# The first MLP product of a hybrid attention block in seven half-size products, with weight sums made by adding DMAs and an order planned inside the kernel

## The chip, the core and the metric

The kernel runs on one core of a Trainium2 chip. The metric is the device time of one launch in microseconds (us). The program is compared with itself before the change. The engines have short names throughout: PE is TensorE (its weight loads are listed apart as PEld), DVE is VectorE, ACT is ScalarE, POOL is GpSimd, and SP is SyncE, which issues most of the transfers.

## The reference

One layer works on 512 tokens of 1024 features, all in float32. The part that the change touches is the last line but one.

```python
def reference(x, positions, g_mix, w_in, ..., g_mlp, w_ff1, w_ff2, g_final):
    h = x
    n = rmsnorm(h, g_mix)
    proj = n @ w_in                     # 512 x 1024 times 1024 x D_IN
    y_gla = gla_branch(...)             # gated linear attention, both directions
    y_mla = mla_branch(...)             # attention over low-rank keys and values, 8 heads
    merged = sigmoid(z_ma) * y_gla + sigmoid(z_mb) * y_mla
    h = h + merged @ w_out              # 1024 x 1024
    m = rmsnorm(h, g_mlp)
    h = h + square(relu(m @ w_ff1)) @ w_ff2   # 1024 x 4096, 4096 x 1024
    return rmsnorm(h, g_final)
```

## The kernel before

Every float32 operand of a product is split into two parts that TensorE takes in one pass each: a high part, which ACT makes by a copy into the type fp32r, and a low part, the rest, which DVE makes by a subtraction (`split`, lines 92 to 94). One product of such pairs is three matmuls, high by high, high by low and low by high (`mm3`, lines 87 to 90):

```python
nc.tensor.matmul(acc, lh, rh, ...)   # L88
nc.tensor.matmul(acc, lh, rl, ...)   # L89
nc.tensor.matmul(acc, ll, rh, ...)   # L90
```

The kernel goes through four stages: the input projections, the two attention branches, the output projection `w_out`, and the MLP. The MLP is the last 315 us. Its input, `m` transposed, lies in eight tiles `mT`, one for each 128 features, each with high and low part for all 512 tokens. The hidden layer has 4096 features, which are 32 tiles of 128. They are worked in four groups (`qd`) of eight tiles.

**First product.** `hidden` (L1480) makes one tile: its weights (1024 x 128, 512 KB) are loaded by SP in pieces of 512 bytes into one of three staging tiles, split into one of four pairs of weight tiles, and multiplied with `mT` in 8 x 3 = 24 matmuls of 128 features by 512 tokens; ACT takes the sum out of PSUM with Relu (L1493). `pair_units` (L1496) takes two such tiles, a pair, squares them on ACT and sorts them by token halves into `px` (tokens 0 to 255) and `qx` (256 to 511) (L1502, L1503).

**Second product.** The square of the hidden layer times `w_ff2` is already made by a scheme of seven products for eight: tokens are halved, the two hidden tiles of a pair are the halves along the summed dimension, and the output columns are halved. Per pair, `left_sums` (L928) makes four sums of the quarter blocks on DVE (L933 to L936), and `split_first`, `split_sum`, `split_corner` split them and the quarter blocks into high and low parts (`ga`; `ghb`, `glb`; `ghc`, `glc`; `gd`). The weight side has four blocks B11, B12, B21, B22 of each group, loaded by `load_w2` on SP; `add_w2` (L986, L988) makes their sums on DVE in place, 32 instructions of 128 x 1024 in the whole MLP, and `prep` (L1448) says which sum is made before which product. Each of the seven block products of a group is 2 row blocks x 4 pairs x 3 = 24 matmuls of 512 columns, in the order `ORDER = (1, 5, 6, 3, 7, 4, 2)`. `add_rows` (L1425, L1427) adds a finished sum from PSUM to the output rows `h` on DVE. In the last group `last_rows` (L1549) works the last products row block by row block, so that the final norm (square on ACT, power -0.5 on POOL, scale, store) of some rows lies under the products of others; the last block is done in two column halves.

**Order.** Most instructions are put in order by the tile scheduler of the language. Where it matters the kernel fixes the order by hand: `traced()` marks a place, `in_program_order` (L110) ties every later instruction of the named engines to the one written ahead of it, and `goes_behind` (L125) moves a marked stretch behind another. Up to the first two hidden tiles (made early, `early[0]` and `early[1]`, while the output projection ends) PE, ACT and DVE go in written order. From line 1686 on, which is the loop over the four groups, the order is the scheduler's, but for the last group's tail.

**Memory.** Tiles come from rings with a fixed number of buffers: `u2` (128 x 512, 29 buffers), `u4` (128 x 2 x 512, 26), weight tiles `wh`, `wl` (4 each), staging `wf` (3). An earlier place in the program has the scans of the linear attention's gates with tiles `rr` (L458, two buffers of their own, L462 the scan).

POOL has little to do in the MLP. In the `w_out` stage it already issues ten transfers that add what they read to what lies in the tile (L984), for the sums of that product's weights.

Of the kernel before, what the change touches and what calls it, by code (L numbers as in the profile page):

```python
# [56 lines left out]
def tile_block(ctx: ExitStack, tc: tile.TileContext, t, out: bass.AP):  # L57
# [128 lines left out]

    class Flipped:
        def __init__(self, gains, name):
            self.gains, self.name = gains, name
            self.out = [u4(f"{name}T{k}") for k in range(KD)]  # L190
            self.banks = {}
# [11 lines left out]
        def evacuate(self, half, ks=range(KD)):  # L203
            tok = slice(half * 256, half * 256 + 256)
            for k in ks:
                hl = self.out[k]
                src = self.banks[half][k % 4][:, (k // 4) * 256 : (k // 4) * 256 + 256]
                split_scaled(hl[:, 0, tok], hl[:, 1, tok], src, self.gains[:, k : k + 1])
# [50 lines left out]
    R = one([P, S], F32, "R")  # L259
# [108 lines left out]

    def gated(acc, name):
# [3 lines left out]
        th = u2(f"t{name}")  # L373
        nc.scalar.activation(th, z, AF.Tanh, scale=0.5)  # L374
        return z, th
# [11 lines left out]
    g2 = [gated(f_accs[2 + x], f"b{x}")[1] for x in range(2)]  # L387
# [47 lines left out]
    class Gates:  # L435
# [492 lines left out]
    def left_sums(px, qx, name, eng):  # L928

        a11, a12, a21, a22 = px[:, 0:HT], px[:, HT:S], qx[:, 0:HT], qx[:, HT:S]  # L930
        y, z = u2(f"y{name}"), u2(f"z{name}")
        s1, s2, s3, s4 = y[:, 0:HT], y[:, HT:S], z[:, 0:HT], z[:, HT:S]
        eng.tensor_tensor(s1, a21, a22, op=ALU.add)  # L933
        eng.tensor_tensor(s2, s1, a11, op=ALU.subtract)  # L934
        eng.tensor_tensor(s3, a11, a21, op=ALU.subtract)
        eng.tensor_tensor(s4, a12, s2, op=ALU.subtract)  # L936
        return y, z

# [47 lines left out]
    def add_w2(dst, x, y, op):  # L986
        for g in range(NP // 2):
            nc.vector.tensor_tensor(wq[dst][g], wq[x][g], wq[y][g], op=op)  # L988

# [18 lines left out]
    def split_w2(x, name):  # L1008
        return [split_part(x, g, name) for g in range(NP // 2)]

    def merged_sums(p, eng):
        px, qx = merged[p]
        a11, a12, a21, a22 = px[:, 0:HT], px[:, HT:S], qx[:, 0:HT], qx[:, HT:S]
        y, z = u2(f"yo{p}"), u2(f"zo{p}")
# [154 lines left out]
    def finish_zb(f, begun):  # L1171
        g2.append(gated(proj_run(begun, xT), f"b{f}")[1])
# [147 lines left out]
    g2.append(gated(zb, "b6")[1])  # L1320
# [18 lines left out]
    g2.append(gated(proj_run(zb, xT, None, range(3, KD)), "b7")[1])  # L1339
# [108 lines left out]
    def prep(m, qd):  # L1448

        more = qd + 1 < NQ  # L1450
        name = f"b{m}_{qd}"
        if m == 1:
            return split_w2(B11, name)
        if m == 2:
            res = split_w2(B21, name)
            if more:
                load_w2(qd + 1, B21)
            return res
        if m == 3:
            return split_w2(B22, name)  # L1460
        if m == 5:
            add_w2(B11, B12, B11, ALU.subtract)
            return split_w2(B11, name)
        if m == 6:
            add_w2(B11, B22, B11, ALU.subtract)
            return split_w2(B11, name)
        if m == 7:
            add_w2(B12, B22, B12, ALU.subtract)
            res = split_w2(B12, name)
            if more:  # L1470
                load_w2(qd + 1, B12)
                load_w2(qd + 1, B22)
            return res
        add_w2(B11, B21, B11, ALU.subtract)
        res = split_w2(B11, name)
        if more:
            load_w2(qd + 1, B11)
        return res

    def hidden(qd, j):  # L1480

        if qd == 0 and j < 2:
            acc = early[j][2]
        elif qd == 0 and j in (2, 3):
            at = traced()
            begun = proj_begin(w1, j * P, f"f{qd}{j}")
            goes_behind((at, traced()), span["norm", NT - 1] if j == 2 else span["evacuate", 1], SPLITTERS)
            goes_behind((at, traced()), span["sums"], SP_ONLY)
            acc = proj_run(begun, mT)
        else:  # L1490
            acc = proj_run(proj_begin(w1, (qd * FQ + j) * P, f"f{qd}{j}"), mT)
        a = u2(f"fa{qd}{j}")
        nc.scalar.activation(a, acc, AF.Relu)  # L1493
        return a

    def pair_units(qd, p, a22):  # L1496

        px, qx = u2(f"px{qd}{p}"), u2(f"qx{qd}{p}")
        for x in range(2):
            a = hidden(qd, 2 * p + x)  # L1500
            c = slice(x * HT, (x + 1) * HT)
            nc.scalar.activation(px[:, c], a[:, 0:HT], AF.Square)  # L1502
            nc.scalar.activation(qx[:, c], a[:, HT:S], AF.Square)  # L1503
        left = {}
        split_first(left, px, f"{qd}{p}")
        y, z = left_sums(px, qx, f"{qd}{p}", nc.vector)
        split_sum(left, y, 5, 6, f"b{qd}{p}")
        split_sum(left, z, 7, 3, f"c{qd}{p}")
# [252 lines left out]
```

## Time and profile before

| | |
|---|---|
| median of three runs | 759.44 us (758.06 to 759.54) |
| the profiled execution | 758.17 us |
| its span, first to last instruction | 756.5 us |
| mean granted TensorE clock | 0.997 |
| busy in the span | PE 745.2, DVE 592.5, ACT 468.1, POOL 128.1 us |

The page of the profile has the engines' busy times, the span cut into 40 slices, the DMA queues (q1 the one with SP's plain transfers, q0 the software queue that POOL issues), the chain of work that ended last, and groups of instructions. A row of a group gives line, engine, operation, names of output and inputs, shapes and count, then the busy time and the mean duration of one in ns, then how long the engine stood idle just before these instructions and what ended that. A row of the timeline gives the start, the duration and the instruction, and in brackets the idle time before it. The shown durations of one engine can overlap: the start of the next instruction tells more of the rate than the duration does.

### The profile page before, as it was taken

How to read it: one execution, taken by the hardware profiler on the slowest of the kernel's cores; microseconds unless marked ns; L12 is line 12 of the kernel's file. 1: busy time of each engine (PE TensorE's matmuls, PEld its weight loads, DVE VectorE, ACT ScalarE, POOL GpSimd, SP SyncE). 2: the span in 40 equal slices, each digit the busy share in tenths (PEclk: the TensorE clock that was granted, in tenths of full speed). 3: DMA queues.
4: the chain of work that ended last, by engine and by line, in shares of the span. 5: the costliest groups of instructions: out<-in, count | busy, mean ns of one | idle time of the engine just before them, and what ended most of it. 6: DMA issues, size and time to landing. Idle time of an engine off the chain costs nothing.

```text
span 756.5 us, 10217 instructions
## 1 busy us (share of the span) xinstructions
PE 745.2 (99%) x3704; PEld 629.7 (83%) x3704; DVE 592.5 (78%) x887; ACT 468.1 (62%) x812; POOL 128.1 (17%) x186
## 2 busy tenths in 40 slices
PE   8999999999999999999999999999999999999996
PEld 7888788888888888899988988888888888888885
DVE  7779899687787787998897787856696578748795
ACT  7556658478767576988866766345544555345644
POOL 1620002031321115036850100000000000000014
PEclk9999999999999999999999999999999999999998
DMA  9832311312234324237998411461126410650003
GB/s 316 255 95 91 128 29 28 84 49 62 59 84 112 60 50 112 73 89 184 273 203 221 133 57 55 139 193 58 56 61 203 127 56 3 206 154 0 29 0 112
DMA packets 97075, 81.30 MB, mean 107 GB/s; under 512 B 15376, under 2 KB 74784, under 8 KB 97024
## 3 DMA queue, kind: packets, MB, share of 16 engines
q1 hardware_dynamic: 93760, 74.07, 33.1%
q0 software_dynamic: 2976, 6.05, 4.3%
q8 instruction: 29, 0.48, 0.3%
q10 hardware_dynamic: 288, 0.52, 0.2%
q14 instruction: 22, 0.18, 0.1%
HBM read 76.96 MB, written 2.10 MB: 105 GB/s over the span
## 4 chain that ended last, share of the span: by engine, by line
PE 93%; ACT 2%; DVE 2%; issue 1%; DMA 1%; POOL 0%; POOLq 0%; ACTq 0%; DVEq 0%
PE f L89 8%; PE f L88 8%; PE f L90 8%; PE gx L88 4%; PE gx L89 4%; PE gx L90 4%; PE first L329 3%; PE tp L1116 2%; PE gz L89 2%; PE gz L88 2%; PE gz L90 2%; PE zb L88 1%; PE za L88 1%; PE zb L90 1%; PE za L90 1%; PE za L89 1%
## 5 line engine op out<-in xcount | busy, mean ns | idle before, releaser
L1700 POOL DMA_DIRECT2D gfin<-in_g_final x1 | 0.6, 623 | 284.1 <-PE f L90 284.1
L988 DVE TENSOR_TENSOR w<-w,w 128x1024 f32<-128x1024 f32 x32 | 38.7, 1219 | 0.3
L1101 ACT ACTIVATE e<-s,top 128x512 f32<-128x512 f32 x32 | 21.9, 685 | 4.4 <-DVE top L1096 3.5
L94 DVE TENSOR_TENSOR pT<-tp,pT 128x512 fp32r<-128x512 f32 x32 | 21.6, 681 | 2.9 <-ACT pT L93 2.9
L1096 DVE TENSOR_REDUCE top<-s 128x1 f32<-128x512 f32 x32 | 21.6, 680 | 2.0 <-PE s L90 1.7
L1427 DVE TENSOR_TENSOR h<-h,gx 128x512 f32<-128x512 f32 x32 | 21.4, 680 | 1.9 <-PE gx L90 1.8
L93 ACT ACTIVATE pT<-tp 128x512 fp32r<-128x512 f32 x32 | 18.8, 592 | 4.3 <-PE tp L1116 4.0
L479 POOL COPY v3f<-rrf 128x4 f32<-128x4 f32 x4 | 2.8, 705 | 109.3 <-DVE rrf L462 109.3
L1116 PE MATMUL tp<-ident,e 128*128 128x128 f32 x128 | 19.3, 274 | 0.3 <-ACT e L1107 0.2
L88 PE MATMUL av<-pT,v 128*128 128x256 f32 x64 | 19.0, 298 | 0.0
L93 ACT ACTIVATE ghb<-y 128x512 fp32r<-128x512 f32 x16 | 10.1, 632 | 14.0 <-DVE y L934 14.0
L1493 ACT ACTIVATE fa<-f 128x512 f32<-128x512 f32 x32 | 18.4, 576 | 0.0
L89 PE MATMUL av<-pT,v 128*128 128x256 f32 x64 | 18.2, 285 | 0.0
L90 PE MATMUL av<-pT,v 128*128 128x256 f32 x64 | 18.2, 284 | 0.0
L1116 PEld LDWEIGHTS tp<-ident,e 128*128 128x128 f32 x128 | 15.1, 140 | 3.7 <-ACT e L1107 1.0
L93 ACT ACTIVATE b_00h<-w 128x1024 fp32r<-128x1024 f32 x7 | 7.4, 1060 | 12.6 <-PE gz L90 6.0
L93 ACT ACTIVATE b_10h<-w 128x1024 fp32r<-128x1024 f32 x7 | 7.4, 1060 | 12.1 <-PE gz L90 6.0
L93 ACT ACTIVATE b_20h<-w 128x1024 fp32r<-128x1024 f32 x7 | 7.4, 1060 | 12.1 <-PE gz L90 6.0
L88 PE MATMUL s<-kbuf,q 96*128 96x512 f32 x32 | 14.1, 441 | 0.0
L374 ACT ACTIVATE tb<-zb 128x512 f32<-128x512 f32 x8 | 5.0, 632 | 14.7 <-DVE zb L372 14.7
L1502 ACT ACTIVATE px<-fa 128x256 f32<-128x256 f32 x32 | 13.4, 418 | 1.0
L984 POOL DMA_DIRECT2D w<-in_w_out x10 | 12.2, 1397 | 6.5 <-DVE bo60l L94 5.3
(1743 smaller groups left out, 2919.1 us busy)
## 6 DMA issues: line engine op xcount, KB each, us to landing
w<-in_w_ff SPq DMA_DIRECT2D x64, 256.0 KB, 3.4
w<-in_w_out POOLq DMA_DIRECT2D x10, 512.0 KB, 8.8
grw<-in_w_in SPq DMA_DIRECT2D x8, 512.0 KB, 9.1
gvw<-in_w_in SPq DMA_DIRECT2D x8, 512.0 KB, 4.5
w<-in_w_out SPq DMA_DIRECT2D x16, 256.0 KB, 5.9
x<-in_xt SPq DMA_DIRECT2D x8, 256.0 KB, 5.3
h<-in_x SPq DMA_DIRECT2D x4, 512.0 KB, 5.1
vw<-in_w_first SPq DMA_DIRECT2D x7, 256.0 KB, 5.4
```

The source lines that it names most:

```text
L88: nc.tensor.matmul(acc, lh, rh, start=start, stop=False, skip_group_check=onto)
L89: nc.tensor.matmul(acc, lh, rl, start=False, stop=False, skip_group_check=onto)
L90: nc.tensor.matmul(acc, ll, rh, start=False, stop=stop, skip_group_check=onto)
L93: nc.scalar.activation(hi, src, AF.Copy)
L94: rest.tensor_tensor(lo, src, raw(hi), op=ALU.subtract)
L329: nc.tensor.matmul(f_accs[i], a[:, i * P : (i + 1) * P], b, start=k == 0 and x == 0, stop=k == KD - 1 and x == 2)
L988: nc.vector.tensor_tensor(wq[dst][g], wq[x][g], wq[y][g], op=op)
L1096: nc.vector.tensor_reduce(top, acc, axis=AX.X, op=ALU.max, negate=True)
L1101: nc.scalar.activation(e, acc, AF.Exp, bias=top, accum_out=tot[:, qt % 2 : qt % 2 + 1])
L1116: nc.tensor.transpose(tp[:, k * P : (k + 1) * P], e[:, k * P : (k + 1) * P], ident)
L1427: nc.vector.tensor_tensor(hc, hc, acc, op=op)
L1493: nc.scalar.activation(a, acc, AF.Relu)
```

## The change

**The first product.** Tiles 0 to 3 stay as they are, but are worked in token halves (`hidden_run`), since `m` transposed now lies in eight tiles by feature half, token half, high and low (`fm.out[j, c]`). The other 28 tiles become seven quads of four tiles. A quad (512 hidden features) uses seven products for eight: the summed dimension (1024) is halved, the tokens are halved, and the four tiles are two pairs of 256 features. One of its products is 2 feature tiles x 4 pieces of 128 x 3 = 24 matmuls of 256 columns. The sums on the token side are made once, by DVE, behind the norm (`summing`: four sums of high and low part, four combinations; `split_m` splits those four). The sums on the weight side are made once per quad: three by transfers that add (`load_add`, issued by POOL) to a loaded block, one more by a DVE addition. PSUM is emptied after every product: m1, m5 and m6 by an ACT copy, m2, m3 and m7 by a DVE addition followed by Relu and Square on ACT, m4 by Relu and Square alone.

**The second product.** Its scheme stays with other signs. The weight sums (`add_w2`, 32 DVE additions) go away; B11 and its follow-ups are made in the tile, by a chain of adding transfers, each issued once the split of the former content has read it. There are 57 adding transfers in the MLP now (two of them ahead of the plan, `w1_sums`), and 59 plain ones in the plan.

**The order.** The loop over the groups is replaced by a list of tasks. PE's order is written out: the first product of a group in pieces between the last products of the odd quad, then group products and products of the next even quad in turn, then the next odd quad. For the other engines, `Plan` makes a list schedule while the kernel is built: each task has a cost (`COST`, and figures for the landing of transfers), a latest start from PE's order, and the tasks that it must follow; at each step the earliest task that can start is taken, the more urgent one first. The instructions are then emitted in that order and tied in it for PE, ACT, DVE and POOL.

**The rest.** The split of tile 3 (with that of tile 2) stands ahead of the second evacuation of `m`. `u2` goes from 29 to 24 buffers, `u4` from 26 to 30; `R` and `rr` move into these rings, and the gates' tanh tiles share one `u4` tile by twos. In the last group the products go 1, 5, 3, 6, 2 (row block 0), 7, 2 (row block 1), 4 (row block 0), 4 (row block 1, in two column halves).

```diff
     def u2(name, dt=F32, shape=(P, S)):
-        return tl(list(shape), dt, "u2", 29, name)
+        return tl(list(shape), dt, "u2", 24, name)
 
     def u4(name, dt=F32R, shape=(P, 2, S)):
-        return tl(list(shape), dt, "u4", 26, name)
+        return tl(list(shape), dt, "u4", 30, name)
...
-    def add_w2(dst, x, y, op):
-        for g in range(NP // 2):
-            nc.vector.tensor_tensor(wq[dst][g], wq[x][g], wq[y][g], op=op)
...
-            rr = tl([P, NT, P + 1], F32, "rr", 2, f"rr{d}")
+            rr = u4(f"rr{d}", F32, (P, NT, P + 1))
...
+    def hidden_run(begun, half, ks=range(KD)):
+        wh, wl, acc = begun
+        c = slice(half * HT, (half + 1) * HT)
+        for k in ks:
+            hi, lo = fm.out[k // 4, half]
+            mm3(acc[:, c], wh[:, k, :], wl[:, k, :], hi[:, k % 4, :], lo[:, k % 4, :], k == 0, k == KD - 1)
+        return acc
...
+    for j in (2, 3):
+        begin_hidden(j)
     at = traced()
     fm.evacuate(1)
...
+        def order(self, head):
...
+                for e in free:
+                    for i in open_[e]:
+                        if e == "PE" and i != pe[0]:
+                            continue
+                        t = max(free[e], ready[i])
+                        rank = (t, late[i], i)
+                        if best is None or rank < best[0]:
+                            best = rank, e, i
...
+                if e in ("SP", "POOL") and lands:
+                    bus = max(bus, end) + 2.6
+                    end = max(bus + 2.0, end + lands)
...
+    COST = {"ACT": {FULL: 0.97, HALFT: 0.52, QUART: 0.32}, "DVE": {FULL: 1.16, HALFT: 0.62, QUART: 0.34}}
...
+    def load(dst, src, key):
+        plan.add("SP", 0.1, lambda: nc.sync.dma_start(dst, src), (), (key,), 4.5)
+
+    def load_add(dst, src, key):
+        plan.add("POOL", 1.27, lambda: nc.gpsimd.dma_start(dst, src, accum_op=ALU.add), (key,), (key,), 9.4)
...
+    wfs = Ring("wf", [stage(KD, P, f"wf{n}") for n in range(3)])
+    hls = Ring("hl", [halves(KD, P, f"hl{n}") for n in range(4)])
...
+        act(FULL, lambda: nc.scalar.activation(wh, src, AF.Copy), (key,), (hkey + (0,),))
+        dve(FULL, lambda: nc.vector.tensor_tensor(wl, src, raw(wh), op=ALU.subtract), (key, hkey + (0,)), (hkey + (1,),))
...
+                dve(FULL, (lambda x=x, hi=hi, lo=lo: nc.vector.tensor_tensor(x, raw(hi), raw(lo), op=ALU.add)),
+                    m_key_of(j, c), (key,))
...
+        combine(A, A, C, ALU.subtract)
+        combine(C, B, C, ALU.subtract)
+        combine(B, B, A, ALU.add)
+        combine(Dd, B, Dd, ALU.subtract)
...
+        def fetch(self):
...
+            load(self.a, self.rows(1, 0), ka)
+            load_add(self.a, self.rows(1, 1), ka)
+
+        def weights(self, m):
...
+            if m == 5:
+                load_add(a, self.rows(0, 0), self.ka)
+                if self.q > 1:
+                    load(self.e, self.rows(1, 0), self.ke)
+                    load_add(self.e, self.rows(0, 0), self.ke)
+            elif m == 6:
+                item, c, key = self.c
+                dve(FULL, lambda: nc.vector.tensor_tensor(a, a, c, op=ALU.add), (self.ka, key), (self.ka,))
...
+        def multiply(self, m):
...
+                for x in range(2):
+                    c = slice(x * HT, (x + 1) * HT)
+                    f = slice(x * P, (x + 1) * P)
+                    for k in range(KD // 2):
+                        mm3(acc[:, c], wh[:, k, f], wl[:, k, f], hi[:, k, :], lo[:, k, :],
+                            begin and x == 0 and k == 0, k == KD // 2 - 1, True)
...
+            if m in (1, 5, 6):
+                act(HALFT, lambda: nc.scalar.activation(x, acc, AF.Copy), (bkey,), (key,))
+            elif m in (2, 3, 7):
+                dve(HALFT, lambda: nc.vector.tensor_tensor(x, acc, x, op=ALU.add), (bkey, key), (key,))
+                self.squared(x, key, -1.0 if m == 7 else 1.0)
+            else:
+                act(HALFT, lambda: nc.scalar.activation(x, acc, AF.Relu, scale=-1.0), (bkey,), (key,))
+                self.squared(x, key, None)
...
+        def prepare(self, m, g):
...
+            if m == 1:
+                self.onto(B11, B12, g)
+            elif m == 5:
+                self.onto(x, B22, g)
+            elif m == 3:
+                self.onto(B22, B12, g)
+            elif m == 6 and not self.last:
+                self.onto(B11, B21, g)
...
+    plan.add("PE", 5.5, second_halves, tuple(("hl", j, x) for j in range(2) for x in range(2)), (("f", 0), ("f", 1)))
+    plains[2].multiply()
+    pair_plain(0)
+    sources = summing()
+    for n, m in enumerate((5, 6, 7, 4)):
+        split_m(m, sources[m], n)
+    plains[3].multiply()
...
+    w.multiply(5)
+    pair_plain(1)
+    for m in (1, 2, 6, 3):
+        w.multiply(m)
+    for qd, g in enumerate(groups):
+        odd = quads[2 * qd + 1]
+        g.multiply(1, 0)
+        odd.multiply(7)
+        g.multiply(1, 1, (2,))
+        odd.multiply(4)
+        second = 5 if g.last else 2
+        g.multiply(second, 0)
+        g.multiply(1, 1, (3,))
+        g.multiply(second, 1)
+        if g.last:
+            break
+        even, odd = quads[2 * qd + 2], quads[2 * qd + 3]
+        for m, between in ((5, 5), (3, None), (6, 1), (7, 2), (4, None)):
+            for x in range(2):
+                g.multiply(m, x)
+            if between:
+                even.multiply(between)
+        for m in (6, 3, 7):
+            even.multiply(m)
+        odd.multiply(5)
+        even.multiply(4)
+        for m in (1, 2, 6, 3):
+            odd.multiply(m)
...
+    plan.emit(0.0)
+    in_program_order(begun, PE_ONLY + SPLITTERS + (mybir.EngineType.Pool,))
```

More of the change, by code (lines that the diff above doesn't have):

```diff
@@ L1445, in flipped @@
         fm.rows(i, ms_rows[i])
[L1448 to L1508, printed above, removed]
-        split_corner(left, qx, a22, p)
-        return left
@@ L1629, in tile_block @@
     wo_product(6)
+    w1_sums = [u4(f"w1s{x}", F32, (P, D)) for x in range(2)]
     fm = Flipped(gvec[:, V_MLP : V_MLP + 8], "m")
-    mT = fm.out
     wo_right[7] = [split_part(B12, 0, "bo7")]
@@ new lines, in evacuate @@
+                if self.last:
+                    if m in (6, 7):
+                        self.finish(upper if m == 6 else lower)
+                    if m == 7 and rb:
+                        self.added(lower, 0, bank)
+                    if m in (2, 4):
+                        self.ended(upper if m == 2 else lower)
+            if m == 2 or m == 3 and self.last:
+                if rbs[-1]:
+                    for a in accs:
+                        mms.back(a)
+            if m == 4:
+                for a in self.xs + self.zs:
+                    ats.back(a)
```

620 lines of the change are left out of this document (492 added, 128 removed).

## The prediction, made before the changed kernel had run

> **What bounds the kernel now.** I read the page first: the engines' busy shares, the slices and the chain that ended last.
>
> ```profile
> span 756.5 us, 10217 instructions
> PE 745.2 (99%) x3704; PEld 629.7 (83%) x3704; DVE 592.5 (78%) x887; ACT 468.1 (62%) x812; POOL 128.1 (17%) x186
> PE   8999999999999999999999999999999999999996
> PEclk9999999999999999999999999999999999999998
> PE 93%; ACT 2%; DVE 2%; issue 1%; DMA 1%; POOL 0%; POOLq 0%; ACTq 0%; DVEq 0%
> ```
>
> TensorE is busy from end to end at the full granted clock, and it makes 93% of the chain. Then I cut the MLP out by stretches (columns after the length: busy PE, PEld, DVE, ACT, POOL; clock; DMA share; GB/s).
>
> ```profile
> 385.00:405.00 20.00, 20.00 (x90) 16.56 (x89) 19.66 (x29) 10.82 (x17) 5.95 (x7) 1.00 1.10 257
> 432.75:747.00 314.25, 314.25 (x1384) 258.87 (x1383) 230.70 (x302) 163.26 (x257) 10.31 (x11) 1.00 0.28 86
> 550.20:632.10 81.90, 81.90 (x361) 67.47 (x361) 58.72 (x77) 40.96 (x63) 0.00 (x0) 1.00 0.34 103
> ```
>
> In the MLP (second row) PE has no gap at all; one group of eight hidden tiles (third row) takes 81.9 us, with DVE busy 72%, ACT 50% and the DMA engines a third. So a cut of PE work is worth its full length there, until something else ends last. The price of the work is read from start to start in the timeline, since the shown durations overlap:
>
> ```profile
> 426.99 0.28 PE L88 MATMUL f<-mT,f00h 128*128 128x256 f32 x1
> ...
> 432.75 0.40 PE L88 MATMUL f<-mT,f02h 128*128 128x512 f32 x1
> ...
> 438.21 0.39 PE L88 MATMUL f<-mT,f03h 128*128 128x512 f32 x1
> ...
> 443.65 0.39 PE L88 MATMUL f<-mT,f04h 128*128 128x512 f32 x1
> ```
>
> Between the first two stand 48 matmuls of 256 columns: 5.76/48 = 0.120 us each. Between the others stand 24 of 512 columns: 5.46 and 5.44 us, 0.227 us each. Half the width costs 53%, not 50%.
>
> **The matmuls.** The hidden tiles 4 to 31 become seven quads. A quad had 4 x 24 = 96 wide matmuls, 96 x 0.2267 = 21.76 us; it gets seven products of 24 narrow ones, 168 x 0.120 = 20.16 us. That is 1.60 us less, and 11.2 us for seven quads. Tiles 2 and 3 keep their arithmetic but run in halves, 48 x 0.120 = 5.76 for 5.44 us: 0.64 us more. Tiles 0 and 1 and the second product keep count and width. Sum for PE: -10.56 us.
>
> The Trainium skill (TensorE: Matmul & The Clock Gate, "Back-to-back issue gap") speaks against the change: in a stream of weight load and matmul pairs it gives some 81 ns at 128 columns and 131 at 512, as the load sets part of the spacing. That makes, between the two, an estimate of 98 ns at 256, three quarters of the wide one: a quad would then lose 168 x 0.098 - 96 x 0.131 = 3.9 us, all of it 27. The rows above disagree: here the narrow one is 53% of the wide one, and both are slower than stated.
>
> **DVE and ACT.** The prices:
>
> ```profile
> L988 DVE TENSOR_TENSOR w<-w,w 128x1024 f32<-128x1024 f32 x32 | 38.7, 1219 | 0.3
> L1427 DVE TENSOR_TENSOR h<-h,gx 128x512 f32<-128x512 f32 x8 | 5.4, 680 | 0.0
> L94 DVE TENSOR_TENSOR glb<-y,ghb 128x512 fp32r<-128x512 f32 x4 | 2.7, 687 | 0.1
> L936 DVE TENSOR_TENSOR z<-px,y 128x256 f32<-128x256 f32 x4 | 1.7, 416 | 0.0
> L1493 ACT ACTIVATE fa<-f 128x512 f32<-128x512 f32 x8 | 4.6, 576 | 0.0
> L93 ACT ACTIVATE b_10h<-w 128x1024 fp32r<-128x1024 f32 x2 | 2.1, 1062 | 0.1
> L1502 ACT ACTIVATE px<-fa 128x256 f32<-128x256 f32 x8 | 3.4, 419 | 0.3
> ```
>
> Away go the 32 weight sums of the second product (38.7 us, first row). A quad brings seven weight splits where four were, one weight sum and three additions out of PSUM; its two row pairs cost as before: 8 x 1.22 + 3 x 0.68 + 2 x (3 x 0.687 + 5 x 0.416) = 20.1 us of DVE. A group (two quads and 14 block products with 14 x 1.22 + 14 x 0.68 = 26.6) makes 66.8 us, against 58.7 shown above, beside 2 x 20.16 + 168 x 0.2267 = 78.4 us of PE: 85%. ACT: a quad has seven splits, eleven passes over 128x512 and two pairs: 7 x 1.06 + 11 x 0.58 + 2 x (3 x 0.62 + 0.40) = 18.3, a group 36.6 + 14 x 1.06 = 51.4, 66%. Both fit beside PE, so on average they cost nothing; if a shortfall came, DVE's margin is 11.6 us a group.
>
> Not on average, but at the entry, DVE is tight. The input of the products must first be summed (eight sums and four splits of 128x1024), while PE runs three plain pieces. What counts here is the spacing on DVE:
>
> ```profile
> 424.50 1.23 DVE L94 TENSOR_TENSOR f02l<-f02f,f02h 128x1024 fp32r<-128x1024 f32 x1 [1.27 <-ACT f02h L93]
> 426.30 3.23 DVE L98 SCALAR_TENSOR_TENSOR mT<-mb,gvec,mT 128x256 fp32r<-128x256 f32 x8 [0.57 <-ACT mT L97]
> 429.80 1.23 DVE L94 TENSOR_TENSOR f03l<-f03f,f03h 128x1024 fp32r<-128x1024 f32 x1 [0.27 <-ACT f03h L93]
> ...
> 437.19 0.42 DVE L935 TENSOR_TENSOR z<-px,qx 128x256 f32<-128x256 f32 x1
> 437.52 0.68 DVE L94 TENSOR_TENSOR ga<-px,ga 128x512 fp32r<-128x512 f32 x1
> ...
> 471.14 0.68 DVE L94 TENSOR_TENSOR glb<-y,ghb 128x512 fp32r<-128x512 f32 x1
> 471.74 1.22 DVE L94 TENSOR_TENSOR b_00l<-w,b_00h 128x1024 fp32r<-128x1024 f32 x1
> 472.88 0.68 DVE L94 TENSOR_TENSOR glc<-z,ghc 128x512 fp32r<-128x512 f32 x1
> ```
>
> From start to start that is 0.33 us after a 128x256 instruction, 0.60 after 128x512 and 1.14 after 128x1024. The split of tile 3 (`f03l`) now stands ahead of the eight evacuations of `mT` and not behind: 1.14 less the 0.57 of idle there shifts them by 0.57, so they end near 430.1. The second halves start when the first evacuation is done, at 426.87 + 3.23/8 = 427.3, 0.3 us later than at 426.99. In the written order the last matmuls of group 0's first product need the low half of pair 3, which is DVE's 55th instruction after 430.1: 24 x 1.14 + 12 x 0.60 + 19 x 0.335 = 40.9 us, so 471.0 without one wait. PE reaches them after 3 x 5.76 + 7 x 2.88 + 2 x 2.72 + 1.36 = 44.2 us, at 471.5. A margin of 0.5 us with DVE full for 41 us: it will not hold, as a low half that waits for its high half costs DVE idle time:
>
> ```profile
> L94 DVE TENSOR_TENSOR b_10l<-w,b_10h 128x1024 fp32r<-128x1024 f32 x2 | 2.5, 1226 | 0.9 <-ACT b_10h L93 0.9
> ```
>
> That is 0.45 us each. If five of the 15 low halves early in this stretch wait so, PE idles 2.25 - 0.5 = 1.7 us, which I take; the ends are 0 (none waits) and 6.2 (all 15 wait, 6.75 - 0.5).
>
> In later groups the same place has a short chain: the odd quad's last product, then Relu, Square and the high half on ACT and the low half on DVE, while PE has one piece of 12 x 0.2267 = 2.72 us.
>
> ```profile
> 439.16 0.61 ACT L93 ACTIVATE ghb<-y 128x512 fp32r<-128x512 f32 x1
> 439.68 0.61 ACT L93 ACTIVATE ghc<-z 128x512 fp32r<-128x512 f32 x1
> ```
>
> At ACT's spacing of 0.52 us the chain takes 3 x 0.52 + 0.68 = 2.2 us; behind a split of 1.06 us on ACT it is 0.6 us late. Three groups: 0 to 2 us (each waits once), I take 1.0.
>
> **The adding DMAs.** Sums that DVE made now come from transfers that POOL issues.
>
> ```profile
> q1 hardware_dynamic: 93760, 74.07, 33.1%
> q0 software_dynamic: 2976, 6.05, 4.3%
> w<-in_w_out POOLq DMA_DIRECT2D x10, 512.0 KB, 8.8
> L984 POOL DMA_DIRECT2D w<-in_w_out x10: 1173/1250/1707, 350.9 to 395.7; - x10
> DMA to landing us min/median/max: 5.6/8.8/12.3
> L1700 POOL DMA_DIRECT2D gfin<-in_g_final x1 | 0.6, 623 | 284.1 <-PE f L90 284.1
> ```
>
> Plain transfers moved 74.07 MB in 33.1% of the span (250 us, 296 GB/s when all engines work): 1.77 us for 512 KB. The software queue, nearly all adding, moved 6.05 MB in 4.3% (32.5 us): 2.82 us for 512 KB. A group period has 16 plain and 14 adding transfers: 28.3 + 39.5 = 67.8 us of 78.4, 86%, for a third now. That fits, and the stretch 385 to 405 above has it worse (share 1.10 while the adding transfers of L984 run, DVE busy 19.66 of 20 us) with PE at 20.00 us: so crowding by itself does not slow PE.
>
> What an adding transfer can delay is the next sum in the same tile. The closest places: in a group, between the fifth product's weights and the sixth's, PE has 5.44 + 2.88 + 5.44 = 13.8 us; the transfer lands after 8.8 and the split takes 1.06 + 1.14: 11.0, spare 2.8. In an odd quad PE has 4 x 2.88 = 11.5; there the runs are 1 KB, so 512 of them (the issue took 623 ns for gfin's 128 runs and 1250 for 256, so 2.5 us): 8.8 + 1.25 + 2.2 = 12.25. It is 0.7 us short unless the weights stand ready early; four pairs of weight tiles allow up to three pieces (8 us) of lead, and I take 3 us. So no wait at the median landing, 1.3 us at the longest (12.3). I take 0, with the ends 0 and 4 us for three odd quads.
>
> **The rest.** POOL's own time (57 issues of 1.25 to 2.5 us) lies beside everything, as POOL is idle 284 us ahead of gfin; it costs only through landing. The pools: the `rr` tiles now come from the shared ring and wait for POOL's low halves of `qsf`, `qsb`:
>
> ```profile
> 153.02 1.06 POOL L94 TENSOR_TENSOR qsb<-qkb,qsb 128x384 fp32r<-128x384 f32 x1
> 161.60 1.36 DVE L462 TENSOR_TENSOR_SCAN rrf<-mf,l 128x128 f32<-128x128 f32 x4
> ```
>
> 7.5 us lie between, so nothing; without that cover a scan would wait up to 1 us on DVE, which PE there does not follow closely. The end keeps its form (a block in two halves, square, power on POOL, scale, store):
>
> ```profile
> 749.53 0.28 PE L90 MATMUL gend<-b_31h,ga 128*128 128x256 f32 x1
> 751.74 0.75 DVE L1541 SCALAR_TENSOR_TENSOR ms<-h,hp,gfin 128x512 f32<-128x512 f32 x1 [0.66 <-POOL hp L184]
> ```
>
> From PE's last matmul to the end of the span 6.9 us; the same three steps stand after it, so 0 (-1 to +1).
>
> **Sum.** The profiled execution took 758.17 us (span 756.5). 758.17 - 10.56 + 0.3 + 1.7 + 1.0 = 750.6. The median of the runs is 759.44 (758.06 to 759.54), 1.3 above the profiled one; between these I put 751.0.
>
> **Rivals.** *VectorE ends last in places* (a wait that takes the place of the matmuls): the 85% and the full entry speak for it, the 11.6 us of margin a group against it. With the entry's upper 6.2 us and the 2 us of the group chains, 758.2 - 10.6 + 0.3 + 6.2 + 2 = 756. *The adding transfers land late; slower.* Place: the odd quads' fifth to sixth product. With a mean landing of 16 us instead of 8.8 each odd quad waits 16 + 1.25 + 2.2 - 11.5 - 3 = 4.9 and each group 16 + 2.2 - 13.8 - 3 = 1.4: 6.3 x 3 = 19, 751 + 19 = 770. It decides from a landing of about 14 us, where 2.9 us per odd quad eats the gain. For it: 86% of the engines' time and up to 12.3 us seen; against it: 8.8 in a stretch as crowded. *The narrow products save nothing.* If changing weights every 256 columns cost 0.1295 us, a quad would take 21.76 as before: 758.2 + 0.6 + 3 = 762. For it only that a product's bank changes halves; against it 48 matmuls in a row at 0.120. *Half the width costs half*, 0.1134 us: a quad takes 168 x 0.1134 = 19.05, 2.71 less, and tiles 2 and 3 cost nothing more: 758.2 - 19.0 + 3 = 742, against the same rows. The Trainium skill's formula for an isolated gap in the section named above (N/2.4 + 2.5 ns, 109 and 216 ns) lies between, near 745 as an estimate; the trace does not bear it out.
>
> **How the numbers follow.** Forecast 0.60, VectorE 0.14, late transfers 0.17, no saving 0.05, half for half 0.04. A measurement can tell about 0.2% (1.5 us) from no change. Faster: 0.60 + 0.04 + 0.13 of VectorE = 0.77; slower: 0.15 of the late transfers and 0.04 of no saving = 0.19; the rest, 0.04, is the same. The forecast's own range is 747.5 (all waits 0: 758.17 - 10.56) to 755 (4 us of late adds on top). The range for 8 in 10 goes from 746.5 to 762.0: it leaves out half for half and most of the late transfers.
>
> **What would show it.** In the changed kernel's profile: narrow matmuls 0.120 us apart; a group of 78 to 80 us; PE idle near 470 to 485 behind DVE's low half of pair 3, and little after; DVE near 85% and the DMA share 0.75 to 0.9 in the MLP; adding transfers landing in 8 to 12 us. I am wrong if PE waits for a low half of a weight whose ACT half waited for a DMA (late transfers), if it idles behind DVE in every group (VectorE), or if the narrow pitch differs from 0.120.

## The result

The changed kernel takes 751.1 us (median of four runs, 750.47 to 751.35) against 759.43 us, a ratio of 0.989 (95% interval 0.988 to 0.991). The forecast was 751.0 us. The profiled execution of the changed kernel took 750.47 us. These are the lines of its page (engines, slices, queues, chain, transfers) that answer to those shown of before:

```profile
span 748.8 us, 11503 instructions
PE 734.6 (98%) x4256; PEld 647.5 (86%) x4256; DVE 617.9 (83%) x920; ACT 503.1 (67%) x831; POOL 197.0 (26%) x243
DMA  9833310212332514326975669998979996997983
q1 hardware_dynamic: 80976, 74.59, 32.8%
q0 software_dynamic: 23856, 35.94, 28.2%
PE 90%; DVE 5%; ACT 3%; issue 1%; DMA 1%; POOL 1%; POOLq 0%; DVEq 0%; ACTq 0%
ms<-in_w_ff POOLq DMA_DIRECT2D x37, 512.0 KB, 8.6
w1s<-in_w_ff POOLq DMA_DIRECT2D x18, 512.0 KB, 9.1
```

PE's busy time fell by 10.6 us, the span by only 7.7. The software queue now moves 35.94 MB; its adding transfers land in 8.6 and 9.1 us at the median. In the MLP the DMA engines are nearly full (the second half of the DMA row). The timeline of PE gives the spacing and the periods:

```profile
433.49 0.28 PE L88 MATMUL f<-m,f02h 128*128 128x256 f32 x1
...
439.25 0.28 PE L88 MATMUL f<-m,f03h 128*128 128x256 f32 x1
...
617.74 0.40 PE L88 MATMUL ab<-hl0h,four 128*128 128x512 f32 x1
...
696.26 0.40 PE L88 MATMUL ab<-hl1h,four 128*128 128x512 f32 x1
...
740.20 0.28 PE L90 MATMUL mb<-hl2h,four 128*128 128x256 f32 x1
```

Tile 2 takes 48 narrow matmuls in 5.76 us, 0.120 each. From one group's first product to the next one's it is 696.26 - 617.74 = 78.52 us (81.9 before). The stretches (columns as before: length; busy PE, PEld, DVE, ACT, POOL; clock; DMA share; GB/s) show a full period and the time behind the entry:

```profile
593.40:671.80 78.40, 78.40 (x506) 71.72 (x505) 62.70 (x83) 49.70 (x66) 17.33 (x14) 1.00 0.91 201
460.00:485.00 25.00, 24.82 (x144) 21.72 (x143) 24.75 (x37) 16.72 (x23) 8.56 (x7) 1.00 1.11 244
```

DVE is busy for 62.70 of 78.40 us in a group, but for 24.75 of 25 at the entry. The profile marks only two waits of PE in the MLP:

```profile
PE mb L90 <- DVE hl1l L1744: 0.6, 1, 0.6
PE mb L88 <- DVE row L1950: 0.2, 1, 0.2
```

### The profile page after: what moved, and what is told of

The parts are those of the page before. It is cut to its first block, busy times and chain, and to the rows that moved or that the text cites. A ratio compares the mean times of both kernels' runs of the same rounds, so it can differ in the third digit from the quotient of the medians.

```text
span 748.8 us, 11503 instructions
## 1 busy us (share of the span) xinstructions
PE 734.6 (98%) x4256; PEld 647.5 (86%) x4256; DVE 617.9 (83%) x920; ACT 503.1 (67%) x831; POOL 197.0 (26%) x243
## 3 DMA queue, kind: packets, MB, share of 16 engines
q1 hardware_dynamic: 80976, 74.59, 32.8%
q0 software_dynamic: 23856, 35.94, 28.2%
## 4 chain that ended last, share of the span: by engine, by line
PE 90%; DVE 5%; ACT 3%; issue 1%; DMA 1%; POOL 1%; POOLq 0%; DVEq 0%; ACTq 0%
PE mb L90 7%; PE mb L88 7%; PE mb L89 7%; PE ab L88 5%; PE ab L89 5%; PE ab L90 5%; PE first L335 3%; PE tp L1109 2%; PE zb L88 1%; PE za L90 1%; PE za L88 1%; PE zb L90 1%; PE za L89 1%; PE zb L89 1%; PE av L89 1%
## 5 line engine op out<-in xcount | busy, mean ns | idle before, releaser
L1699 POOL DMA_DIRECT2D ms<-in_w_ff x37 | 47.0, 1363 | 111.2 <-DVE hl3l L1744 34.1
L1699 POOL DMA_DIRECT2D w1s<-in_w_ff x16 | 20.1, 1262 | 93.6 <-DMA w1s<-in_w_ff 32.8
L1420 DVE TENSOR_TENSOR h<-h,ab 128x512 f32<-128x512 f32 x48 | 31.0, 682 | 2.4 <-PE ab L90 2.4
L1744 DVE TENSOR_TENSOR hl3l<-ms,hl3h 128x1024 fp32r<-128x1024 f32 x13 | 15.9, 1223 | 5.3 <-ACT hl3h L1743 5.3
L1109 PE MATMUL tp<-ident,e 128*128 128x128 f32 x128 | 19.3, 274 | 0.4 <-ACT e L1100 0.2
L1744 DVE TENSOR_TENSOR hl1l<-ms,hl1h 128x1024 fp32r<-128x1024 f32 x12 | 14.7, 1223 | 5.1 <-ACT hl1h L1743 5.1
L1743 ACT ACTIVATE hl3h<-ms 128x1024 fp32r<-128x1024 f32 x13 | 13.7, 1052 | 7.3 <-PE ab L90 4.6
L88 PE MATMUL mb<-four,hl0h 128*128 128x256 f32 x64 | 18.2, 284 | 0.2 <-DVE row L1950 0.2
L1978 ACT ACTIVATE row<-row 128x512 f32<-128x512 f32 x28 | 17.7, 631 | 0.8
L90 PE MATMUL av<-pT,v 128*128 128x256 f32 x64 | 18.1, 284 | 0.0
L90 PE MATMUL mb<-four,hl0l 128*128 128x256 f32 x64 | 18.1, 283 | 0.0
L89 PE MATMUL mb<-four,hl0h 128*128 128x256 f32 x64 | 18.1, 283 | 0.0
L1743 ACT ACTIVATE hl1h<-ms 128x1024 fp32r<-128x1024 f32 x12 | 12.7, 1054 | 7.6 <-PE ab L90 4.9
```

Source lines behind the costliest of these rows:

```text
L88: nc.tensor.matmul(acc, lh, rh, start=start, stop=False, skip_group_check=onto)
L89: nc.tensor.matmul(acc, lh, rl, start=False, stop=False, skip_group_check=onto)
L90: nc.tensor.matmul(acc, ll, rh, start=False, stop=stop, skip_group_check=onto)
L1109: nc.tensor.transpose(tp[:, k * P : (k + 1) * P], e[:, k * P : (k + 1) * P], ident)
L1420: nc.vector.tensor_tensor(hc, hc, acc, op=op)
L1699: plan.add("POOL", 1.27, lambda: nc.gpsimd.dma_start(dst, src, accum_op=ALU.add), (key,), (key,), 9.4)
```

## The experiments

The profiles here differ by up to 1.7 us in the first 15 us of the program (the start of the input projection), where all these programs are alike, and, unless an edit reaches further back, by hardly anything from there to the MLP. The medians have a limit too: the changed kernel measured 751.1 us at first and 751.76 in a later series. So, beside the medians, the profiles are compared by one stretch: from the first matmul of tile 2 to the end of the span. It is 756.5 - 432.75 = 323.75 us before and 748.8 - 433.49 = 315.31 us after the change, 8.44 less.

### The end of the kernel

From PE's last matmul to the end of the span there are 748.8 - 740.48 = 8.3 us (its start, 740.20, and 0.28), 1.6 more than before (756.5 - 749.81 = 6.7). The timeline of the changed kernel shows what stands there:

```profile
737.16 1.29 POOL L1468 TENSOR_TENSOR row<-h,w1s 128x512 f32<-128x512 f32 x1
737.37 1.10 DVE L1480 SCALAR_TENSOR_TENSOR hp<-hp 128x1 f32<-128x1 f32 x1 [0.79 <-ACT sz L1472]
738.55 0.55 POOL L1484 TENSOR_TENSOR hp<-hp,mhalf 128x1 f32<-128x1 f32 x1
739.13 0.75 DVE L1488 SCALAR_TENSOR_TENSOR sz<-h,hp,w1s 128x512 f32<-128x512 f32 x1 [0.66 <-POOL hp L1484]
739.80 0.68 DVE L1420 TENSOR_TENSOR h<-h,ab 128x512 f32<-128x512 f32 x1
740.40 0.42 DVE L2130 TENSOR_TENSOR h<-mb,h 128x256 f32<-128x256 f32 x1
...
741.74 0.42 DVE L2130 TENSOR_TENSOR h<-mb,h 128x256 f32<-128x256 f32 x1
```

The addition for row block 2 (L1420) waits in DVE's queue behind the scaling of row block 1 (L1488), which waits for POOL; the last addition (L2130) begins at 741.74, 1.3 us after its matmuls.

```diff
-            plan.add("POOL", 1.5, lambda: out_gained(i), (("row", i, 1, "h"), self.gain_key), (key, ("hp", i)))
+            plan.add("POOL", 2.3, lambda: out_gained(i), (("row", i, 1, "h"), self.gain_key), (key, ("hp", i)))
```

> Edit: the planner's figure for the row product with the final gain on POOL goes from 1.5 to 2.3; its only effect is at the end, where VectorE adds the finished sums of row block 2 before it scales row block 1 (the reverse of now). Theory (the end lost 1.6 us against the kernel before, 8.3 us from the last matmul to the end of the span instead of 6.7, because VectorE's queue stood behind POOL there): the end shortens by 1.2 to 1.6 us, time 749.5 to 749.9. Rival (the stores set the end whatever VectorE does): 751.1, no change.

Measured: 750.51 us (750.21 to 750.76), 0.6 less and not the 1.2 to 1.6 of the theory. The profiled execution had lost 1.7 us in the first 15 us. The two kernels then ran side by side:

> The changed kernel once more, beside the next run on the same chip. The two profiles so far differ by up to 1.7 us in the time up to the first product, and by nothing from there to the MLP: 750.5 to 752, with a span of 735.2 us from the first product's first matmul on.

> The kernel with the other order at the end once more, beside the changed kernel on the same chip. Theory (the end is 1.5 us shorter, and what hid it in the first comparison was the time up to the first product): 1.0 to 1.5 us below the run before, 749.5 to 750.5. Rival (no gain): equal to it within 0.3.

Measured: 751.76 us (750.77 to 752.77) for the changed kernel and 750.62 (750.23 to 751.07) with the other order at the end. By the stretch from tile 2 (e11 first, e12 second):

```profile
span 749.8 us, 11503 instructions
...
434.71 0.28 PE L88 MATMUL f<-m,f02h 128*128 128x256 f32 x1
...
741.32 0.28 PE L90 MATMUL mb<-hl2h,four 128*128 128x256 f32 x1
```

```profile
span 749.1 us, 11503 instructions
...
435.38 0.28 PE L88 MATMUL f<-m,f02h 128*128 128x256 f32 x1
...
742.16 0.28 PE L90 MATMUL mb<-hl2h,four 128*128 128x256 f32 x1
```

315.09 and 313.72 us: 1.4 less, as expected. The gain is all at the end: from the last matmul to the end of the span it is 749.8 - 741.60 = 8.2 us in the first and 749.1 - 742.44 = 6.7 in the second, as before the change. The medians differ by 1.1 us. The planner's figure had been too small for what POOL does there, and so it ordered DVE wrongly. This is the fastest version of the study that leaves out no work: 0.9885 of the kernel before (0.987 to 0.990).

### Two more instructions at the entry

Two of the four sums of high and low part (`twice`) get one more instruction, which changes no value.

```diff
-                dve(FULL, (lambda x=x, hi=hi, lo=lo: nc.vector.tensor_tensor(x, raw(hi), raw(lo), op=ALU.add)),
-                    m_key_of(j, c), (key,))
+                def both(x=x, hi=hi, lo=lo, twice=(c, j) in ((0, 0), (1, 1))):
+                    nc.vector.tensor_tensor(x, raw(hi), raw(lo), op=ALU.add)
+                    if twice:
+                        nc.vector.tensor_tensor(x, x, x, op=ALU.max)
+
+                dve(FULL, both, m_key_of(j, c), (key,))
```

> Edit: two additional VectorE instructions of 128x1024 (the maximum of a sum with itself) in the sums at the entry of the MLP. Theory (VectorE has no spare time there: no idle from 430 to 485 us, and the low half of pair 3 ends at 472.5 just as TensorE starts on it): TensorE waits 2 x 1.14 = 2.3 us more, time 753.2 to 753.5. Rival (the entry has slack, as TensorE waited only 0.4 us there): 751.1 to 751.5.

Measured: 754.09 us (752.74 to 755.15), 3.0 more, 0.6 above the theory's range. PE's additional waits in that run, at 470 and 456 us:

```profile
PE mb L88 <- DVE row L1954: 1.4, 1, 1.4
PE mb L88 <- ACT row L1952: 0.8, 1, 0.8
```

The stretch is 752.3 - 434.70 = 317.60, 2.29 more than 315.31: both instructions at their full 1.14 us. So there is no spare time on VectorE from the norm to the first group product; that PE hardly waits there is a tie and not a margin.

### More work for VectorE in the groups

```diff
+        twice = len(splits) > 14 and len(splits) % 4 == 0
...
+            nc.vector.tensor_tensor(wl, src, raw(wh), op=ALU.subtract)
+            if twice:
+                nc.vector.tensor_tensor(wl, raw(wl), raw(wl), op=ALU.max)
```

> Edit: behind every fourth weight split after the entry VectorE makes one more instruction of 128x1024 (23 in the MLP, 26 us). Theory (a group needs 62.6 us of VectorE beside 78.4 us of TensorE, so 6 or 7 more, 7.4 us, are covered): 751.1 to 752.1. Rival (VectorE is in truth the bound through its chains with ScalarE): up to 26 us more, above 760.

Measured: 758.94 us (757.83 to 760.22), 7.8 more: the theory missed, and the rival's range (above 760) too. PE's three largest waits in its MLP, where all its waits add up to 5.1 us:

```profile
PE ab L88 <- DVE h L1420: 2.6, 3, 1.7
PE mb L90 <- DVE hl1l L1748: 1.4, 1, 1.4
PE mb L88 <- DVE row L1958: 1.1, 3, 0.7
```

They are short waits for an addition out of PSUM or a low half that now stands behind one more instruction. The mean leaves 15.7 us a group, but not where the additional work falls. The next run told whether this is the order's fault:

```diff
-        dve(FULL, low, (key, hkey + (0,)), (hkey + (1,),))
+        plan.add("DVE", 1.16 * (2 if twice else 1), low, (key, hkey + (0,)), (hkey + (1,),))
```

> Edit: the additional VectorE instructions of the run before that had 23 of them, with their cost told to the planner, so that the order is made for them. Theory A (the 7 us that they cost came from an order made for other durations; the spare time of VectorE is there): 751 to 753. Theory B (VectorE's spare time cannot be used, since its instructions come in chains with ScalarE and with TensorE's results): 757 to 759 as before.

Measured: 754.8 us (752.95 to 755.18), 3.7 more than the changed kernel. Between both theories: about half of the cost was an order made for other durations, the other half stays. 26 us of work at a told cost take 3.7 us, untold 7.8 (2.6 and 7.0 by the stretch from tile 2). PE's waits in the MLP are then 3.2 us.

### The second product's weight sums by VectorE again

```diff
-            load_add(dst, self.rows(y, g), key)
+            item, part, pkey = staged(self.rows(y, g), 2)
+            dve(FULL, lambda: nc.vector.tensor_tensor(dst, dst, part, op=ALU.add), (key, pkey), (key,))
+            wfs.back(item)
```

> Edit: the weight sums of the second product are made by VectorE again (36 instructions of 128x1024), from plain loads into the three shared staging tiles; the adding transfers remain only for the quads. Theory (VectorE has 15.8 us of spare time a group and would need 8 x 1.14 = 9.1): 751 to 754, where the 3 is for the staging tiles being shared. Rival (without the adding transfers VectorE ends last): 36 x 1.14 = 41 us more work of which most shows, above 770.

Measured: 775.85 us (774.63 to 776.33), 24.7 more and slower than before the change. The rival was right on the size. But the stretches tell where:

```profile
475.00:485.00 10.00, 6.39 (x17) 4.54 (x16) 8.48 (x10) 4.04 (x6) 1.28 (x1) 0.66 0.48 105
556.00:636.00 80.00, 79.26 (x509) 72.18 (x507) 70.89 (x90) 49.71 (x67) 7.77 (x6) 1.00 0.76 198
709.00:727.00 18.00, 8.24 (x45) 6.80 (x44) 17.85 (x26) 10.50 (x16) 0.00 (x0) 0.82 0.61 184
```

In a middle group DVE does 70.89 of 80 us and PE loses 0.7. Right behind the entry (first row) and at the last group (third row, DVE 17.85 of 18) PE loses 3.6 and 9.8 us, and the granted clock falls to 0.66 and 0.82 besides. The longest wait of PE in the last group, 7.26 us, ends with ACT's high half `hl0h`; ACT had stood 2.26 us for a DVE addition out of PSUM, which came behind two of the weight sums in DVE's queue. So the additions were put back into the middle groups alone:

```diff
+            if self.qd in (0, NQ - 1):
+                load_add(dst, self.rows(y, g), key)
+                return
```

> Edit: the weight sums of the second product by VectorE again, as in the run with 36 of them, but only in groups 1 and 2 (16 instructions); groups 0 and 3 keep the adding transfers. Theory (in that run PE lost its time where VectorE was full already, 4 us and a slower clock behind the entry and 10 us in the last group, and some 2 us in groups 1 and 2 at 88% of VectorE): 752 to 755. Rival (each VectorE addition costs the same wherever it stands, 24.7 us / 36 = 0.69 us): 751.1 + 11 = 762.

Measured: 754.91 us (754.26 to 755.61), 3.2 more than the changed kernel on the same chip (751.76) and within the theory's range. If the costs simply add, 16 of the 36 additions cost 0.2 us each, the other 20 some 1.1 us each ((24.7 - 3.2) / 20). The adding transfers earn their place at the two ends of the MLP, where VectorE is full. In both runs the additional loads also share the three staging tiles; how much of the cost is theirs was not separated. In the run with 36, ACT waits for a load into such a tile twice, 1.50 us at 496 us and 2.01 at 745, at neither of the two places.

### Later landing

`late` is true for the quads' sums alone; the second run has 8 * 2 in place of 8 * 1.

```diff
+            for w in range(8, 8 + 8 * 1 * late, 8):
+                nc.gpsimd.dma_start(dst[0:1, 0, 0:w], zeros[:, 0:w], accum_op=ALU.add)
+            nc.gpsimd.dma_start(dst, src, accum_op=ALU.add)
```

> Edit: ahead of each of the 19 adding transfers of the quads in the plan POOL issues a small transfer that adds zeros to 8 elements of the same tile, and the large one waits for its landing. Estimate: 4 us later each, since the shortest landing of an adding transfer seen is 5.6 us from issue, part of it the transfer. Theory (the odd quads' spare time is about 2.5 us by the prediction's working): three odd quads wait 1.5 us each, time 755 to 757. Rival (the transfers are issued so early that 4 us more are hidden): 751 to 752.

> Edit: as the run before, with two such small transfers in a row, some 8 us later each. Theory (spare time of 2.5 us): three odd quads wait 5.5 us each, and some transfers of the groups behind them in POOL's queue too, time 766 to 772. Rival (hidden): 751 to 753. The point from which landing decides lies between the two runs if this one alone is slower by more than 10 us.

Measured: 764.74 us (763.79 to 766.22) and 817.3 (816.49 to 823.24), 13.6 and 66.2 more: all the ranges were missed, as the first run alone is already slower by more than 10 us. The delay was larger than estimated. POOL's timeline of the first run:

```profile
527.91 0.82 POOL L1703 DMA_DIRECT2D w1s<-zeros  x1 [1.44 <-DVE hl0l L1751]
532.09 1.32 POOL L1704 DMA_DIRECT2D w1s<-in_w_ff  x1 [3.35 <-DMA w1s<-zeros]
532.85 1.41 POOL L1703 DMA_DIRECT2D ms<-zeros  x1
538.72 1.32 POOL L1704 DMA_DIRECT2D ms<-in_w_ff  x1 [4.46 <-DMA ms<-zeros]
```

4.2 and 5.9 us from the small issue to the large one; over the run the small transfers land 1.9 to 9.4 us after their issue, median 5.4. With the 8.8 us at which the adding transfers of the plan land (median) that puts the quads' sums at 8.8 + 5.4 = 14.2 us after the first issue. ACT's waits of the same run say who feels it, the high halves of the weights:

```profile
ACT hl3h L1750 <- DMA w1s<-in_w_ff: 14.8, 5, 4.3
ACT hl1h L1750 <- DMA w1s<-in_w_ff: 14.6, 4, 4.9
ACT hl1h L1750 <- DMA ms<-in_w_ff: 7.4, 2, 5.4
```

In the changed kernel ACT waits for transfers of the MLP only 1.2 us in all:

```profile
ACT hl2h L1743 <- DMA ms<-in_w_ff: 0.8, 1, 0.8
ACT hl3h L1743 <- DMA w1s<-in_w_ff: 0.4, 1, 0.4
```

PE's own waits add up to 9.8 us in the first run and 49 in the second, where the mean granted clock falls to 0.966 besides (0.996 in the changed kernel). They are mostly named after evacuations (`h`, `row`), which stand in ACT's and DVE's queues with these splits. While POOL waits for a small transfer, the transfers of the second product behind it in its queue are late too. That may be why the first run costs more than the prediction's working of late transfers gives at 14.2 us (3.15 us per odd quad, 9.5); the two delays were not separated.

### Without the list schedule

```diff
-            return sorted(range(n), key=lambda i: begun[i])
+            return list(range(n))
...
-    in_program_order(begun, PE_ONLY + SPLITTERS + (mybir.EngineType.Pool,))
+    in_program_order(begun, PE_ONLY)
```

> Edit: the tasks are emitted in the order in which they are written, and only TensorE is tied to it; the language's tile scheduler orders ScalarE, VectorE and POOL, as it did for the MLP before. Theory (VectorE has so little spare time that its order decides): above 765. Rival (any order that follows TensorE's will do, and the list schedule adds nothing): 751 to 754.

Measured: 779.22 us (775.7 to 779.75), 28.1 more. The edit reaches further back than its text says: it also unties ScalarE, VectorE and POOL in the `w_out` stage and the norm. By the stretch from tile 2, 777.9 - 437.32 = 340.58 us, 25.3 us of the loss lie in the MLP. PE's waits there add up to 14.7 us, and the mean granted clock is 0.987 (0.996 in the changed kernel). The largest are 9.1 us in three places for an evacuation by ACT:

```profile
PE mb L88 <- ACT row L1948: 9.1, 3, 3.4
```

The same instructions in this other order make the change a loss of 20 us.

### Less work for TensorE

```diff
-                        mm3(acc[:, c], wh[:, k, f], wl[:, k, f], hi[:, k, :], lo[:, k, :],
-                            begin and x == 0 and k == 0, k == KD // 2 - 1, True)
+                        first = begin and x == 0 and k == 0
+                        nc.tensor.matmul(acc[:, c], wh[:, k, f], hi[:, k, :], start=first, stop=False, skip_group_check=True)
+                        nc.tensor.matmul(acc[:, c], wl[:, k, f], hi[:, k, :], start=False, stop=k == KD // 2 - 1, skip_group_check=True)
```

> Edit: the quads' products leave out the third matmul of each three (low part of the token side), 56 of 168 a quad, so their result lacks that part; 392 narrow matmuls less, 47.0 us of TensorE. Theory (behind TensorE stand VectorE with 62.6 us and the DMA engines with about 0.9 x 78.4 = 70.6 us a group, and TensorE would need 65.0): 8 to 13 us saved a group, 27 to 45 us in all at most, and less where VectorE is full: 715 to 735. Rival (TensorE alone sets the time): 704 to 706.

Measured: 733.73 us (733.04 to 734.96), 18.0 less than the changed kernel on the same chip, of 47.0 us of matmuls taken away, and within the theory's range. A middle stretch and PE's largest waits:

```profile
520.00:600.00 80.00, 75.54 (x445) 66.89 (x444) 69.70 (x97) 56.91 (x80) 17.32 (x14) 0.96 1.01 221
```

```profile
PE mb L1934 <- DVE row L1951: 11.2, 6, 3.7
PE mb L1934 <- ACT row L1949: 4.7, 4, 1.8
```

TensorE alone no longer sets the time: its waits in the MLP add up to 19.3 us, most of them for PSUM banks that DVE and ACT empty, with the DMA engines full. The mean granted clock falls from 0.996 to 0.985 besides. The 47.0 us brought 18.0; what the first few of them would bring, no run shows.

## Why the prediction was right, step by step

**The matmuls (-10.56 us): right.** The narrow spacing is 0.120 us, a group period 78.52 us against 78.4 worked out. From tile 2's first matmul to the last one it is 306.71 us against 316.78, 10.07 less; PE's two waits (0.8 us) are more than the 0.5 that is missing, so the matmuls themselves came out 0.3 shorter than worked out. The lower prices in the Trainium skill (TensorE: Matmul & The Clock Gate, "Back-to-back issue gap") would have made the change a loss; half the width cost 53% here as in the trace of before, so the trace decides.

**The entry (+0.3 and +1.7, from 0 to 6.2).** The 0.3 is right: tile 2 starts 0.74 us later, and 0.42 of these stand ahead of the second halves, which begin at 427.41 us (426.99 before). The 1.7 is too much; rows of DVE and PE:

```profile
471.88 0.69 DVE L1825 TENSOR_TENSOR m<-row,m 128x512 fp32r<-128x512 f32 x1
472.45 0.39 PE L88 MATMUL ab<-hl3h,m 128*128 128x512 f32 x1
...
472.90 0.39 PE L90 MATMUL ab<-hl3h,m 128*128 128x512 f32 x1
```

The low half of pair 3 (first row) is DVE's 55th instruction behind the evacuations, as forecast. It is done at about 472.5, where 471.0 was worked out without a wait; PE begins with pair 3 at 472.45, first takes the low half at 472.90 (L90), and doesn't wait. The step that failed is the five waits of DVE for ACT of 0.45 us each: the only wait of DVE for ACT that its timeline marks between 430 and 485 us is one of 0.19, presumably since the order has another instruction ready wherever a high half is not. The list schedule is not needed for that: in the run without it DVE waits only 0.46 us for ACT between 430 and 474 us. The low half comes 1.5 us later than worked out: 0.3 of it is DVE's later start, 0.2 that wait, and about 1 us gaps too short to be marked. The tie itself was read rightly, as the two more instructions show: they cost 2.29 of 2.28 us.

**The chains in the groups (+1.0): not seen.** PE waits 0.6 us at one place in the groups, at 536 us, for a low half of a quad's weights and not for pair 3.

**The adding transfers (0, from 0 to 4): right.** ACT waits 1.2 us for them in all, and the low half that PE waits 0.6 us for has a high half that ACT began without a marked wait. A term was too large: the issue of a quad's adding transfer was taken at 2.5 us, and POOL's issues at L1699 take 1.26 and 1.36 us (means of `w1s` and `ms`). That landing decides at about 14 us is borne out only roughly: at 8.6 to 9.1 us nothing shows, and at some 14.2 us for the quads' sums alone the loss is 13.6 where 9.5 was worked out. So the gain is gone somewhat earlier than forecast; no run lies between.

**The end (0, from -1 to +1): wrong.** It costs 1.6 us. "The same three steps stand after it" holds, but what fails is that the work ahead of them stayed as it was: the last group's order changed, and DVE's queue stood behind POOL. The run with the other order takes it back. (The 6.9 us of the forecast is about the time from the start of the last matmul; from its end it is 6.7.)

**The sum.** Waits and shift of 3.0 us were forecast, 1.1 us came (0.3 and the two waits of 0.8); the end added 1.6 where 0 stood, and 0.4 lies ahead of the second halves, within the 1.7 us by which the starts of the profiles differ. That the forecast meets the median to 0.1 us is in part these errors cancelling; term by term it was right to about 2 us.

**VectorE's margin: wrong in kind.** "DVE's margin is 11.6 us a group" is a mean, and the mean was even better (15.7): the 66.8 us a group were added up from shown durations, which overlap, and the trace has 62.70. The runs showed that it can't be spent just anywhere: two more instructions at the entry cost their full length, and 26 us more in the groups cost 7.8 us unplanned and 3.7 planned. Such small disturbances already come near the 756 of the rival that VectorE ends last. The prediction was saved by the order, whose worth it had not priced: in the one run without the list schedule the time was 779 us.

## What to carry to other kernels

When an engine stands at 80% beside a full TensorE, ask for each stretch and each queue whether the spare time lies where the work comes; add one instruction there and see whether it shows in full. A product scheme that saves TensorE 1.4% needs the other engines' order planned with measured durations: here the order was worth some 25 us in the MLP against one other order, and the matmuls 10.6, and one wrong figure in the planner cost 1.4. Compare profiles from a mark behind the first loads, so that the start of the program doesn't hide a microsecond.

## What the runs showed of the hardware

**Short VectorE instructions beside POOL.** In the end's timeline above DVE's 128x1 instruction (L1480) takes 1.10 us and ends with POOL's 128x512 product (737.16 + 1.29 = 738.45); the same line takes 0.16 us at 741.27, where POOL is idle. The second profile of the changed kernel has the same: 1.10 us, again to the end of POOL's product. The Trainium skill (SBUF — State Buffer, "SBUF: two separate sides") says that the two engines share a pair of ports which one instruction holds to its end, a VectorE instruction with two inputs in SBUF (as this one) among them; the trace agrees.

**The clock after two waits.** In the run with VectorE's sums PE stood 2.21 and 1.40 us at one place, with one matmul between (columns as in the timeline before):

```profile
477.72 0.51 PE L88 MATMUL mb<-hl2h,m 128*128 128x512 f32 x1 [2.21 <-ACT hl2h L1743]
479.63 0.80 PE L89 MATMUL mb<-hl2l,m 128*128 128x512 f32 x1 [1.40 <-DVE hl2l L1744]
480.23 0.63 PE L90 MATMUL mb<-hl2h,m 128*128 128x512 f32 x1
480.65 0.63 PE L88 MATMUL mb<-hl2h,m 128*128 128x512 f32 x1
...
485.16 0.40 PE L90 MATMUL ab<-hl0h,gl 128*128 128x512 f32 x1
```

After them wide matmuls come 0.43 us apart for some 5 us, then 0.23 again: the two waits of 3.6 us cost about 2.2 us more. The Trainium skill (TensorE: Matmul & The Clock Gate, "What's actually happening") gives half the clock after an idle window of about 3.4 us; here two shorter waits with a matmul between them sufficed.

**Adding transfers.** They moved 35.94 MB in 28.2% of 16 engines' span, 170 GB/s when all work, against 304 for the plain ones (74.59 MB in 32.8%): 3.1 us for 512 KB where 2.8 were taken from before. With the DMA engines' share at 0.91 they still land in 8.6 to 9.1 us.
